# Down of two feed-forward layers by one step of Strassen's algorithm

## The chip, the cores and the metric

The kernel runs on one core of one Trainium2 chip. Its five queues of instructions are TensorE (PE, matrix products into PSUM; PEld is its loading of the stationary operand), VectorE (DVE), ScalarE (ACT), GpSimd (POOL) and SyncE (SP). In this kernel SP issues all DMAs, in the order in which the program has them, and an issue that has to wait for another engine or a transfer holds up those behind it. The metric is the time of one execution on the device in microseconds (us), as the median of several executions.

## The reference

Two layers on 1024 tokens of 1024 features, all in float32. Each layer has a token mixer (layer 0 forgetting attention, layer 1 an S5 state space) and a feed-forward part, each inside two RMSNorms:

```python
x = x + rmsnorm(m, mix_post_gain[i])
h = rmsnorm(x, ffn_pre_gain[i])
x = x + rmsnorm(swiglu(h, ffn_w_gate[i], ffn_w_up[i], ffn_w_down[i]), ffn_post_gain[i])

def swiglu(h, w_gate, w_up, w_down):
    return (jax.nn.silu(h @ w_gate) * (h @ w_up)) @ w_down
```

D_FF is 2816, that is 22 blocks of 128. The last product, g @ w_down, is what the change rewrites: 1024 tokens x 2816 features times 2816 x 1024, once per layer.

## The kernel before

**Precision.** A float32 operand is split in two of type fp32r: a rounded part h, written by ACT (`split`, L253), and the rest l = x - h, by DVE (L254). A product is then three matmuls, h*h, h*l and l*h (`mm3`, L270 to L274), each 128 x 128 stationary by 128 x 512 moving into one of eight PSUM banks.

**Loading ahead.** The operands that come from DRAM stand in one list (`plan`): source, shape, and the rings of pages that the parts go to. `take` returns an item's parts; it splits (`_cut`) the item taken and the next one, and each split sends the loads of the two items behind it (`_load`, L231). A ring is a short list of 4 KB pages in SBUF that are used in turn, so a load waits until its page's last reader is done. `raw` holds weights before the split (three pages in Down), `gr` the loaded g (two pages), `wdh`/`wdl` and `gh`/`gl` the parts. The order on each engine is not that of the code: a scheduler sets it from priorities and its own costs when the program is built, so SP's order, too, is one that it chose.

**gate_up** computes g = silu(h Wg) * (h Wu), transposed (features on partitions, tokens along the row), for two feature blocks 2p and 2p + 1 at a time. It takes them as the two halves of a Strassen step of its own with 14 steps of 12 matmuls (L756). The pages `s` hold g's blocks (z[0]) and `up` the partial sums (z[1]). After steps 11 and 13 the two blocks go to the DRAM tensor g_d (L813, L815).

**Down** (L825) runs over the two token halves (hf). In each it goes through the 11 pairs of feature blocks: the pair's two weight blocks of 128 x 1024 and its g (128 x 2 x 512) are taken, and for each of four token blocks tb and two column halves three matmuls per feature block add into bank 2 tb + nh. That is 48 matmuls a pair, 1056 a layer. The last two pairs are taken together, so that the four token blocks end one after another; ACT and DVE copy a block's two banks to a page m (L838, L839), and `finish` is called on it: `fin0` in layer 0 (norm, residual, store to x2, and the next norm's rstd; L1464 to L1473), `fin1` in layer 1 (a product with the gain, rstd, and one operation that scales and adds the residual x, which is loaded from x3, L1510; L1518 writes x and L1519 stores it to the output).

**Beside Down of layer 0.** `s5_rot` makes eight rotation tables for layer 1's mixer on POOL: per table six products (L1119 to L1121) on one page s5w0 and a scratch page s5w1, and a store to rot_d by SP (L1109). One table's code stands beside each of the first eight groups of the first half. Ahead of them `s5_params` does its last work beside gate_up; its last store, T_d (L1051), goes out from the scratch page that the first rot writes next. In the second half Down also takes eight rows of s5_w_in, which ACT and POOL split (L1224, L1225). After Down come `s5_in`'s transposes of the finished blocks (L1236).

Of the kernel before, what the change touches and what calls it, by code (L numbers as in the profile page):

```python
# [9 lines left out]
F32 = mybir.dt.float32  # L10
# [149 lines left out]
class Trunk:  # L160
    def __init__(self, ctx, tc, A, out):
        self.tc, self.nc, self.A, self.out = tc, tc.nc, A, out
        nc = self.nc
        mk = lambda name, bufs, **k: ctx.enter_context(tc.tile_pool(name=name, bufs=bufs, **k))
        self.cst = mk("cst", 1)
        self.hp = mk("hp", 4)
        self.pp = mk("pp", 1)
        self.sm = mk("sm", 4)
        self.ps = mk("ps", 1, space=bass.MemoryType.PSUM).tile([P, 8 * 512], F32, name="ps")
# [119 lines left out]
    def rstd(self, src, junk, cuts=1, out=None):  # L289
        nc = self.nc  # L290
        V = nc.vector
        ss, n = self.small("ss"), D // cuts
        for i in range(cuts):
            s = slice(i * n, i * n + n)
            part = self.small("sp") if i else ss
            nc.scalar.activation(junk[:, s], src[:, s], AF.Square, accum_out=part)
            if i:
                V.tensor_add(ss, ss, part)
# [389 lines left out]
    def ffn_plan(self, i, g_d, extra=()):  # L688

        A = self.A  # L690
        Wg, Wu, Wd = A["ffn_w_gate"][i], A["ffn_w_up"][i], A["ffn_w_down"][i]
        for p in range(NF // 2):
            for W in (Wg, Wu):
                for f in (2 * p, 2 * p + 1):
                    self.plan(self.cols(W, f * P)[:2] + (None, None, None))
        for hf in range(2):
            for p in range(NF // 2):
                for f in (2 * p, 2 * p + 1):
                    self.plan(self.rows(Wd, f * P, ("wdh", "wdl")))
                src = g_d[2 * p * P:(2 * p + 2) * P, hf * 512:hf * 512 + 512].rearrange("(a p) t -> p a t", p=P)  # L700
                self.plan((src, (P, 2, 512), ("gh", "gl"), None, None, "gr"))
                if hf:
                    self.plan(*extra[p:p + 1])

    def gate_up(self, B, g_d, beside=iter(()), when=lambda p, s: False):

# [63 lines left out]
        for p in range(n):  # L770
# [11 lines left out]
            for s in range(14):  # L782
# [42 lines left out]
    def down(self, finish, beside=iter(()), extra=0, last=2):  # L825
# [3 lines left out]
        nc, R = self.nc, self.R  # L829
        n = NF // 2  # L830
        groups = [[p] for p in range(n - last)] + [list(range(n - last, n))]
        for hf in range(2):
            m = {}

            def out(tb):
                t = m[tb] = R("m")
                with self.tc.high_priority(AHEAD):
                    nc.scalar.copy(t[:, 0:512], self.bank(2 * tb, 1, (P, 512)))  # L838
                    nc.vector.tensor_copy(t[:, 512:1024], self.bank(2 * tb + 1, 1, (P, 512)))  # L839

            for ps in groups:
                w = []
                for p in ps:
                    w.append((self.take(), self.take()))
                    w[-1] += (self.take(),)
                for tb in range(4):
                    t = slice(tb * P, tb * P + P)
                    for p, (w0, w1, g) in zip(ps, w):
                        for f, (wh, wl) in enumerate((w0, w1)):
                            for nh in range(2):  # L850
                                c = slice(nh * 512, nh * 512 + 512)
                                self.mm3(self.bank(2 * tb + nh, 1, (P, 512)), g[0][:, f, t], g[1][:, f, t], wh[:, c],
                                         wl[:, c], p == f == 0, p == n - 1 and f == 1)
                    if len(ps) > 1:
                        out(tb)
                if hf == 0:
# [519 lines left out]
def trunk(ctx: ExitStack, tc: tile.TileContext, A, out):  # L1376
# [36 lines left out]
    g_d = [T.dram(f"g{i}_d", [FF, D]) for i in range(2)]  # L1413
# [13 lines left out]
    R.set(pw=[29], R1=[30], R2=[31], s5t0=[34], s5t1=[32], s5t2=[33], s5w0=[28], s5w1=[32], fx=[4, 33], fj=[6, 34],  # L1427
# [34 lines left out]
    ys = []  # L1462

    def fin0(tb, m):  # L1464
# [8 lines left out]
        ys.append((m, T.rstd(m, R("fj"), out=T.rr5[:, tb:tb + 1])))  # L1473
# [12 lines left out]
    ins = [T.s5_in(tb, *ys[tb]) for tb in range(8)]  # L1486
# [34 lines left out]
    T.down(fin1)  # L1521
# [29 lines left out]
```

## Time and profile before

| | us |
|---|---|
| median of 3 runs | 2506.91 (2504.44 to 2507.9) |
| the profiled execution | 2504.19 |
| its span | 2502.4 |
| mean granted TensorE clock | 0.994 of full speed |

The busy time of each engine and its count of instructions stand in the page's first part, which the next section shows. In a window's line each engine has its busy time and, in brackets, how many of its instructions the window holds; then come the granted TensorE clock, the mean busy share of the 16 DMA engines and GB/s. In a group of instructions, busy time and mean ns stand behind the first bar, and behind the second the idle time ahead of them with what ended it. In the waits, an engine's line, what it waited for, total us, number of times and the longest. "SPq" rows are issues of DMAs.

### The profile page before, as it was taken

To read this page: it belongs to the slowest core of one execution; us is meant where nothing else is said; L and a number is where in the kernel's file an instruction comes from. 1 tells how busy PE (TensorE), PEld (TensorE's weight loads), DVE (VectorE), ACT (ScalarE), POOL (GpSimd) and SP (SyncE) were. 2 spreads that over 40 slices of the span, in tenths; PEclk is the share of its full clock that TensorE was granted. 3 is DMA by queue.
4 is the path that set the end of the run, shared out by engine and by line. 5 is a ranking of instruction groups with operands and counts; after the bars stand their busy time and mean duration, and the time that the engine had idled before them with its cause. 6 is when DMAs were issued, how large, how long until landed. Compare 5 with 4: busy or idle time off the path is not lost.

```text
span 2502.4 us, 31357 instructions
## 1 busy us (share of the span) xinstructions
PE 2421.5 (97%) x11748; PEld 1984.6 (79%) x11748; DVE 1576.0 (63%) x2803; ACT 1153.7 (46%) x1951; POOL 545.2 (22%) x447
## 2 busy tenths in 40 slices
PE   7999999999998999999999999899999999999998
PEld 5777777777787888888777878788878888888887
DVE  6877787778778865656536355763785554543444
ACT  5766676666655334343316343332453333332322
POOL 3323321223100035465782102420000000000100
PEclk9999999999999999999999999999999999999999
DMA  4121111211343323333547622443323223235452
GB/s 131 49 59 43 43 43 51 59 43 43 109 145 85 110 81 116 114 99 105 186 162 255 210 76 83 144 153 112 127 84 100 84 76 93 85 104 177 156 203 93
DMA packets 228872, 268.35 MB, mean 107 GB/s; under 512 B 31392, under 2 KB 176992, under 8 KB 228720
## 3 DMA queue, kind: packets, MB, share of 16 engines
q1 hardware_dynamic: 228720, 266.35, 33.3%
q8 instruction: 92, 1.51, 0.2%
q14 instruction: 60, 0.49, 0.1%
HBM read 205.95 MB, written 60.36 MB: 106 GB/s over the span
## 4 chain that ended last, share of the span: by engine, by line
PE 72%; DVE 12%; ACT 6%; POOL 5%; DMA 2%; issue 2%; SPq 0%; DVEq 0%; ACTq 0%; POOLq 0%
PE ps L756 30%; PE ps L272 11%; PE ps L273 11%; PE ps L274 11%; PE ps L567 2%; PE ps L586 1%; DVE wl L254 1%; DVE ps L548 1%; POOL s5w L1066 1%; DVE ptl L571 1%; DMA T_d<-s5w 1%; DVE p L434 1%; POOL s5w L1121 1%; POOL s5w L1120 1%; ACT pth L570 1%
## 5 line engine op out<-in xcount | busy, mean ns | idle before, releaser
L756 PE MATMUL ps<-B,ah 128*128 128x512 f32 x1056 | 329.4, 393 | 2.0 <-ACT hold L106 1.6
L273 PE MATMUL ps<-wdl,gh 128*128 128x512 f32 x704 | 275.0, 391 | 2.9 <-DVE wdl L254 2.9
L272 PE MATMUL ps<-wdh,gh 128*128 128x512 f32 x704 | 274.1, 390 | 3.0 <-ACT wdh L253 3.0
L274 PE MATMUL ps<-wdh,gl 128*128 128x512 f32 x704 | 274.2, 390 | 1.2 <-DVE gl L254 1.2
L254 DVE TENSOR_TENSOR wdl<-raw,wdh 128x1024 fp32r<-128x1024 f32 x88 | 119.7, 1362 | 219.1 <-ACT wdh L253 213.0
L756 PEld LDWEIGHTS ps<-B,ah 128*128 128x128 f32 x1056 | 200.3, 190 | 45.1 <-ACT hold L106 1.8
L756 PE MATMUL ps<-ops,ah 128*128 128x512 f32 x704 | 218.1, 391 | 0.0
L272 PE MATMUL ps<-hT,wh 128*128 128x512 f32 x512 | 207.2, 405 | 9.1 <-DVE pt L409 4.3
L555 POOL TENSOR_SCALAR Pt<-Pt,ri 128x128 f32<-128x128 f32 (+7 forms) x128 | 118.2, 925 | 414.7 <-DVE ri L554 326.3
L756 PE MATMUL ps<-B,al 128*128 128x512 f32 x528 | 207.0, 392 | 0.0
L253 ACT CAST wdh<-raw 128x1024 fp32r<-128x1024 f32 x88 | 92.5, 1051 | 248.1 <-PE ps L274 163.4
L273 PE MATMUL ps<-hT,wh 128*128 128x512 f32 x512 | 203.5, 397 | 0.0
L274 PE MATMUL ps<-hT,wl 128*128 128x512 f32 x512 | 202.7, 396 | 0.0
L1514 POOL TENSOR_TENSOR y<-m,s 128x1024 f32<-128x1024 f32 x6 | 15.3, 2552 | 817.1 <-DVE m L839 812.8
L273 PEld LDWEIGHTS ps<-wdl,gh 128*128 128x128 f32 x704 | 132.5, 188 | 31.8 <-DVE wdl L254 4.3
L272 PEld LDWEIGHTS ps<-wdh,gh 128*128 128x128 f32 x704 | 132.6, 188 | 31.7 <-ACT wdh L253 3.9
L274 PEld LDWEIGHTS ps<-wdh,gl 128*128 128x128 f32 x704 | 132.6, 188 | 29.0 <-DVE gl L254 1.7
L756 PEld LDWEIGHTS ps<-ops,ah 128*128 128x128 f32 x704 | 131.4, 188 | 28.8 <-issue 1.7
L727 DVE TENSOR_TENSOR al<-raw,ah 128x1024 fp32r<-128x1024 f32 x88 | 117.8, 1339 | 52.6 <-ACT ah L726 52.1
L726 ACT CAST ah<-raw 128x1024 fp32r<-128x1024 f32 x88 | 92.6, 1052 | 125.6 <-PE ps L756 114.6
L571 DVE TENSOR_TENSOR ptl<-ps,pth 128x512 fp32r<-128x512 f32 (+1 forms) x192 | 106.3, 554 | 54.9 <-ACT pth L570 49.6
L756 PE MATMUL ps<-ops,al 128*128 128x512 f32 x352 | 137.0, 389 | 0.0
(322 smaller groups left out, 5645.2 us busy)
## 6 DMA issues: line engine op xcount, KB each, us to landing
raw<-in_ffn_w_down_dram SPq DMA_DIRECT2D x88, 512.0 KB, 4.6
raw<-in_ffn_w_gate_dram SPq DMA_DIRECT2D x44, 512.0 KB, 3.9
raw<-in_ffn_w_up_dram SPq DMA_DIRECT2D x44, 512.0 KB, 4.3
g_d<-s SPq DMA_DIRECT2D x44, 512.0 KB, 3.4
gr<-g_d SPq DMA_DIRECT2D x44, 512.0 KB, 5.2
raw<-in_fox_w_in_dram SPq DMA_DIRECT2D x32, 512.0 KB, 4.2
x<-in_x_dram SPq DMA_DIRECT2D x16, 512.0 KB, 6.2
An<-negc SPq DMA_DIRECT2D x16, 512.0 KB, 4.7
```

The source lines that it names most:

```text
L253: self.nc.scalar.copy(h, src)
L254: self.lsub.tensor_sub(l, src, f32(h))
L272: mm(ps, lh, rh, start=start, stop=False)
L273: mm(ps, lh, rl, start=False, stop=False)
L274: mm(ps, ll, rh, start=False, stop=stop)
L434: nc.vector.tensor_sub(l, qs[r], f32(h))
L555: nc.gpsimd.tensor_scalar(p[:, :nk], p[:, :nk], ri, 1.0, op0=ALU.mult, op1=ALU.mult)
L567: nc.tensor.transpose(p2[:, i], p[:, (g + i) * P:(g + i + 1) * P], self.ident)
L571: nc.vector.tensor_sub(dl, p2[:, 0:n], f32(dh))
L726: nc.scalar.copy(h, src)
L727: V.tensor_sub(l, src, f32(h))
L756: nc.tensor.matmul(bank, x[:, k], y, start=start and k == i == 0, stop=True, skip_group_check=True)
```

## The change

The sum over 22 blocks is cut in halves (blocks p and p + 11), and so are tokens and columns; of the eight half products seven are left, in Winograd's form. gate_up now takes blocks p and p + 11 as its pair and stores, besides parts of g itself, the sums and differences that the seven products need: g_d becomes four DRAM tensors. Down runs four phases. The first three take two products at a time, X in the even banks and Y in the odd ones, 24 matmuls a pair; the fourth takes the last product alone, on Y, two pairs at a time (24 matmuls again, the last step one pair). 7 x 132 = 924 matmuls a layer. Between phases ACT and DVE move sums from PSUM to the eight pages m; X goes on adding through the first three phases. The differences of weights are made on DVE from raw rows (`sums`): three 128 x 512 operations a pair in the second phase, two in the third. The `rot` code stands beside every second pair of the first phase and the steps of the fourth; the s5_w_in rows are taken in the third.

```diff
-        for p in range(NF // 2):
+        n = NF // 2
+        for p in range(n):
             for W in (Wg, Wu):
-                for f in (2 * p, 2 * p + 1):
+                for f in (p, p + n):
                     self.plan(self.cols(W, f * P)[:2] + (None, None, None))
-        for hf in range(2):
-            for p in range(NF // 2):
-                for f in (2 * p, 2 * p + 1):
-                    self.plan(self.rows(Wd, f * P, ("wdh", "wdl")))
-                src = g_d[2 * p * P:(2 * p + 2) * P, hf * 512:hf * 512 + 512].rearrange("(a p) t -> p a t", p=P)
-                self.plan((src, (P, 2, 512), ("gh", "gl"), None, None, "gr"))
-                if hf:
-                    self.plan(*extra[p:p + 1])
...
+            def cut(raw):
+                b = self.cut[-1]
+                t, h, l = self.R("t"), self.R("wdh", sh, F32R), self.R("wdl", sh, F32R)
+                if second:
+                    V.tensor_sub(t[:, hi], b[:, hi], b[:, lo])
+                    V.tensor_sub(t[:, lo], raw[:, hi], t[:, hi])
+                    V.tensor_sub(t[:, hi], raw[:, lo], t[:, lo])
+                else:
+                    V.tensor_sub(t[:, lo], raw, b[:, hi])
+                    V.tensor_sub(t[:, hi], b[:, hi], b[:, lo])
+                self.split(h, l, t.rearrange("p (a c) -> p a c", a=2))
+                return h, l
...
+        for p in range(n):
+            ga(0, p)
+            self.plan((W2[p][:, :, lo], sh, op, None, None))
+        for p in range(n):
+            ga(1, p)
+            self.plan(rows(p), rows(p + n)[:2] + (sums(1, 1), None, None))
+        for p in range(n):
+            ga(2, p)
+            self.plan(rows(p), (W2[p][:, 1, hi], (P, 512), sums(1, 0), None, None), *extra[p:p + 1])
+        for p in range(0, n, 2):
+            ga(3, p)
...
                 elif s == 11:
                     times(0, hi)
-                    nc.sync.dma_start(g_d[2 * p * P:2 * p * P + P, :], z[0][0])
+                    g0, g1, q0, q1 = *z[0], *z[1]
+                    V.tensor_add(q0[:, hi], g0[:, hi], g1[:, hi])
+                    V.tensor_sub(q0[:, lo], g0[:, lo], g0[:, hi])
+                    nc.sync.dma_start(g_d[0][p][:, lo], g0[:, lo])
+                    nc.sync.dma_start(g_d[1][p][:, hi], g1[:, hi])
+                    nc.sync.dma_start(g_d[2][p], q0)
                 elif s == 13:
-                    nc.sync.dma_start(g_d[2 * p * P + P:2 * p * P + 2 * P, :], z[0][1])
+                    V.tensor_sub(q1[:, lo], q0[:, hi], g0[:, lo])
+                    V.tensor_sub(q1[:, hi], g1[:, lo], q1[:, lo])
+                    nc.sync.dma_start(g_d[0][p][:, hi], g1[:, lo])
+                    nc.sync.dma_start(g_d[1][p][:, lo], q1[:, lo])
+                    nc.sync.dma_start(g_d[3][p], q1[:, hi])
...
+        for ph in range(3):
+            for p in range(n):
+                g = self.take()
+                if ph:
+                    self.take()
+                w = self.take()
+                for tb in range(4):
+                    mm(X[tb], g, w, 0, tb, p == ph == 0)
+                    mm(Y[tb], g, w, 1, tb, p == 0)
+                if ph == 2 and p < extra:
+                    self.take()
+                if ph == 0 and p % 2 == 0:
+                    next(beside, None)
+            with self.tc.high_priority(AHEAD):
+                for tb in range(4):
+                    a, b = m[tb], m[4 + tb]
+                    if ph == 0:
+                        nc.scalar.copy(a[:, lo], X[tb])
+                        V.tensor_add(a[:, lo], a[:, lo], Y[tb])
...
+        for tb in range(4, 8):
+            finish(tb, m[tb])
+        js = list(range((n + 1) // 2))
+        for i, grp in enumerate([[j] for j in js[:-last]] + [js[-last:]]):
+            ops = [(self.take(), self.take()) for j in grp]
+            next(beside, None)
+            for tb in range(4):
+                for j, (g, w) in zip(grp, ops):
+                    for k in range(min(2, n - 2 * j)):
+                        mm(Y[tb], g, w, k, tb, False)
+                if len(grp) > 1:
+                    with self.tc.high_priority(AHEAD):
+                        V.tensor_add(m[tb][:, hi], m[tb][:, hi], Y[tb])
+                    finish(tb, m[tb])
...
-    R.set(raw=[0, 1, 2], gr=[35, 36], gh=[3, 37, 18], gl=[5, 7, 29], wdh=rg(8, 13), wdl=rg(13, 18), m=rg(19, 27), s=[27])
-    T.down(fin0, T.s5_rot(), 8)
+    R.set(raw=[0, 1, 2, 14], gr=[35, 36], t=[15, 16], gh=[3, 37, 18], gl=[5, 7, 29], wdh=rg(8, 11), wdl=rg(11, 14),
+          m=rg(19, 27), s=[27])
+    T.down(fin0, beside=T.s5_rot(), extra=8)
...
-    R.set(raw=[0, 1, 2], gr=[32, 33], gh=[35, 36, 37], gl=[7, 8, 9], wdh=rg(10, 15), wdl=rg(15, 19) + [20], m=rg(22, 30))
+    R.set(raw=[0, 1, 2, 19, 20], gr=[32, 33, 14], t=[15, 16], gh=[35, 36, 37], gl=[7, 8, 9], wdh=rg(10, 13) + [17],
+          wdl=[13, 18, 21, 34], m=rg(22, 30), x=[3, 4], y=[5, 6], y4=[5, 6, 15, 16], j=[31], s=[30])
```

In layer 1 a new `begin1` computes the first column half of the last four blocks' gain product (POOL) and square sum (ACT) ahead of their end; fin1 then does the second half, with the gain product on POOL for blocks 4 to 7 and on DVE for 0 to 3, and x and its store in two halves for block 3, which now ends last. Blocks 4 to 7 are finished beside the fourth phase, in both layers, and s5_in takes the blocks in that order.

Three places of the built program follow. The first is SP's queue where gate_up of layer 0 ends and Down begins. A name's number grows with the place in the code, so of the g loads before the change gr_10865 is pair 0's and gr_10883, gr_10958 and gr_11033 those of pairs 1 to 3. Before:

```order
L231 DMA gr_10865<-g_d 128x2x512
L813 DMA g_d<-s_10606 128x1024
L231 DMA gr_10883<-g_d 128x2x512
L1051 DMA T_d<-s5w_1034_10840 128x1024
L231 DMA raw_11027<-in_ffn_w_down_dram 128x1024
L815 DMA g_d<-s_10607 128x1024
L231 DMA raw_10952<-in_ffn_w_down_dram 128x1024
L1109 DMA rot_d<-s5w_1049_10933 128x1024
L231 DMA gr_10958<-g_d 128x2x512
```

Now, where gr_10962, gr_10970, gr_10982 and gr_11027 are pairs 0, 1, 2 and 3:

```order
L857 DMA g_d<-up_10698 128x512
L1118 DMA T_d<-s5w_1034_10933 128x1024
L232 DMA gr_10970<-g_d 128x1024
L856 DMA g_d<-s_10696 128x512
L858 DMA g_d<-up_10698 128x512
L335 DMA s_12415<-in_ffn_post_gain_dram 128x1024
L1176 DMA rot_d<-s5w_1054_11008 128x1024
L232 DMA gr_10962<-g_d 128x1024
L232 DMA gr_11027<-g_d 128x1024
L1176 DMA rot_d<-s5w_1068_11089 128x1024
L232 DMA gr_10982<-g_d 128x1024
L1176 DMA rot_d<-s5w_1082_11170 128x1024
```

The loads of pairs 0 and 3 now stand behind the first rot store, pair 2's behind the second; in the rows that follow each further rot store is followed by the g load of one pair, 4 to 9, and the eighth also by the first weight row of the second phase, raw_11381. Pair 0's page (35) is also that of up_10698, so its load stands behind L857 and L858 in any case.

The second place is DVE at the end of that first phase, where before it only went on with splits (gl and wdl, L254). gl_11267 and wdl_11297 are pair 8's, t_11430 is the second phase's first difference. Now:

```order
L255 TENSOR_TENSOR wdl_11261<-raw_11219,wdh_11260 128x1024
L255 TENSOR_TENSOR gl_11267<-gr_11225,gh_11266 128x1024
L709 TENSOR_TENSOR t_11430<-raw_11381 128x512
L255 TENSOR_TENSOR wdl_11297<-raw_11264,wdh_11296 128x1024
L255 TENSOR_TENSOR gl_11303<-gr_11270,gh_11302 128x1024
```

The difference L709, which needs raw_11381, is ahead of pair 8's wdl.

The third place is SP's queue at the very end, stores of finished blocks (out_dram) and loads of x. Before, with x_19836 for the last block and x_19818 for the one ahead of it:

```order
L1510 DMA x_19818<-x_d 128x1024
L1519 DMA out_dram<-x_19800 128x1024
L1510 DMA x_19836<-x_d 128x1024
L1519 DMA out_dram<-x_19818 128x1024
L1519 DMA out_dram<-x_19836 128x512 x2
```

and now, with x_20195 for the last block and x_20161 for the one ahead:

```order
L1584 DMA x_20161<-x_d 128x1024
L1591 DMA out_dram<-x_20127 128x1024
L1591 DMA out_dram<-x_20161 128x1024
L1584 DMA x_20195<-x_d 128x1024
L1591 DMA out_dram<-x_20195 128x512 x2
```

The last block's x load has moved behind the store of the block ahead of it.

More of the change, by code (lines that the diff above doesn't have):

```diff
@@ L286, in new_hT, with rstd @@
                 for _ in range(2)]
-    def rstd(self, src, junk, cuts=1, out=None):
+    def rstd(self, src, junk, part=None, out=None):
         nc = self.nc
         V = nc.vector
[L292 to L298, printed above, removed]
+        ss = self.small("ss")
+        s = slice(0 if part is None else 512, D)
+        nc.scalar.activation(junk[:, s], src[:, s], AF.Square, accum_out=ss)
+        if part is not None:
+            V.tensor_add(ss, ss, part)
         rt = self.small("rt")
@@ new lines, in ffn_plan, with rows, sums @@
+        V, sh, lo, hi, op = self.nc.vector, (P, 2, 512), slice(0, 512), slice(512, 1024), ("wdh", "wdl")
+        def rows(r):
+            return (Wd[r * P:r * P + P, :], (P, D), None, None, None)
+        def sums(first, second):
+            def cut(raw):
[10 more added lines that the diff above has]
+                return h, l
+            return cut
@@ new lines, in ga @@
+        def ga(x, k0=None):
+            src = g_d[x][k0].rearrange("p (a c) -> p a c", a=2) if x < 3 else g_d[3][k0:min(k0 + 2, n)].rearrange("k p c -> p k c")
+            m = src.shape[1]
+            self.plan((src, (P, m, 512), ("gh", "gl"), None, None, "gr"))
+        for p in range(n):
[4 more added lines that the diff above has]
+            self.plan(rows(p), rows(p + n)[:2] + (sums(1, 1), None, None))
@@ L823, in gate_up, with down @@
                     next(beside, None)
-    def down(self, finish, beside=iter(()), extra=0, last=2):
+    def down(self, finish, begin=lambda tb, m: None, beside=iter(()), extra=0, last=3):
         nc, R = self.nc, self.R
+        V = nc.vector
         n = NF // 2
[L831 to L845, printed above, removed]
-                for tb in range(4):
[L847 to L856, printed above, removed]
-                    next(beside, None)
-                elif ps[0] < extra:
-                    self.take()
-            for tb in range(4):
-                finish(4 * hf + tb, m[tb])
@@ new lines, in down, with mm @@
+        lo, hi = slice(0, 512), slice(512, 1024)
+        m = {tb: R("m") for tb in (4, 5, 6, 7, 0, 1, 2, 3)}
+        X, Y = ([self.bank(2 * tb + i, 1, (P, 512)) for tb in range(4)] for i in (0, 1))
+        def mm(bank, g, w, j, tb, start):
+            t = slice(tb * P, tb * P + P)
+            for i, (x, y) in enumerate(((g[0], w[0]), (g[0], w[1]), (g[1], w[0]))):
+                nc.tensor.matmul(bank, x[:, j, t], y[:, j], start=start and i == 0, stop=True, skip_group_check=True)
+        for ph in range(3):
[4 more added lines that the diff above has]
+                w = self.take()
+                for tb in range(4):
+                    mm(X[tb], g, w, 0, tb, p == ph == 0)
[3 more added lines that the diff above has]
+                if ph == 0 and p % 2 == 0:
+                    next(beside, None)
+            with self.tc.high_priority(AHEAD):
[4 more added lines that the diff above has]
+                        V.tensor_add(a[:, lo], a[:, lo], Y[tb])
+                    elif ph == 1:
+                        nc.scalar.copy(a[:, hi], X[tb])
+                        V.tensor_copy(b[:, lo], Y[tb])
+                    else:
+                        nc.scalar.copy(b[:, hi], Y[tb])
+                        V.tensor_add(b[:, lo], b[:, lo], X[tb])
+                        V.tensor_add(b[:, hi], b[:, hi], X[tb])
@@ new lines, in down @@
+        for tb in range(4, 8):
[4 more added lines that the diff above has]
+            next(beside, None)
+            for tb in range(4):
+                for j, (g, w) in zip(grp, ops):
[5 more added lines that the diff above has]
+                    finish(tb, m[tb])
+            if i == 0:
+                for tb in range(4):
+                    begin(tb, m[tb])
@@ L864, in exp @@
+        run(beside)
     def exp(self, x, out, tmp):
@@ L1412, in trunk @@
     T.plan(*wos[:4], T.cols(Wi, 3 * D + 7 * P), act[0], *wos[4:], *act[1:])
-    g_d = [T.dram(f"g{i}_d", [FF, D]) for i in range(2)]
+    g_d = [[T.dram(f"g{i}{x}_d", [NF // 2, P, D if x < 3 else 512]) for x in range(4)] for i in range(2)]
     T.ffn_plan(0, g_d[0], [T.rows(A["s5_w_in"][0], k * P, T.s5_w_in_cut(k)) for k in range(8)])
@@ L1460, in trunk @@
     gp = []
-    ys = []
+    ys = {}
     def fin0(tb, m):
@@ L1472, in fin0 @@
         nc.sync.dma_start(x2_d[:, tb, :], m)
-        ys.append((m, T.rstd(m, R("fj"), out=T.rr5[:, tb:tb + 1])))
+        ys[tb] = m, T.rstd(m, R("fj"), out=T.rr5[:, tb:tb + 1])
     R.widen("raw", 19)
@@ L1481, in trunk @@
     T.slots = (0, 2)
-    R.set(raw=[0, 1, 2], gr=[35, 36], gh=[3, 37, 18], gl=[5, 7, 29], wdh=rg(8, 13), wdl=rg(13, 18), m=rg(19, 27), s=[27])
-    T.down(fin0, T.s5_rot(), 8)
+    R.set(raw=[0, 1, 2, 14], gr=[35, 36], t=[15, 16], gh=[3, 37, 18], gl=[5, 7, 29], wdh=rg(8, 11), wdl=rg(11, 14),
+          m=rg(19, 27), s=[27])
+    T.down(fin0, beside=T.s5_rot(), extra=8)
     T.U = [R("U", (P, 8, 8, 16)) for _ in range(8)]
     T.tab, T.st, T.M, T.pe = {}, {}, [], None
-    ins = [T.s5_in(tb, *ys[tb]) for tb in range(8)]
+    ins = [T.s5_in(tb, *ys[tb]) for tb in (4, 5, 6, 7, 0, 1, 2, 3)]
     run(T.s5_tables(0))
```

31 lines of the change are left out of this document (18 added, 13 removed).

## The prediction

> **What bounds the kernel now.** I read the page first, then the two stages that the change rewrites, as windows, then who waited there.
>
> ```profile
> span 2502.4 us, 31357 instructions
> PE 2421.5 (97%) x11748; PEld 1984.6 (79%) x11748; DVE 1576.0 (63%) x2803; ACT 1153.7 (46%) x1951; POOL 545.2 (22%) x447
> 1220.80:1470.70 249.90, 242.72 (x1058) 199.06 (x1058) 126.45 (x137) 92.37 (x124) 103.49 (x64) 0.99 0.56 192
> 2255.00:2494.00 239.00, 239.00 (x1055) 197.58 (x1054) 95.70 (x106) 76.19 (x89) 15.31 (x6) 1.00 0.46 156
> ```
>
> PE is the bound, and the two windows are Down of layer 0 and of layer 1. A matmul is listed with some 390 ns, but these overlap: layer 1 puts 1055 of its 1056 into 239.0 us, so one costs 0.2267 us. At that pitch Down takes 239.4 us. Layer 1 reaches that; layer 0 takes 249.9, 10.5 more. SP's queue and POOL say why:
>
> ```profile
> SPq L1109 <- POOL s5w L1121: 65.5, 8, 9.7
> 1232.02 0.32 SPq L1109 DMA_DIRECT2D rot_d<-s5w  x1
> 1232.43 0.39 SPq L231 DMA_DIRECT2D gr<-g_d  x1
> ...
> 1285.71 0.32 SPq L1109 DMA_DIRECT2D rot_d<-s5w  x1
> 1286.13 0.37 SPq L231 DMA_DIRECT2D raw<-in_ffn_w_down_dram  x1
> ...
> 1304.91 0.32 SPq L1109 DMA_DIRECT2D rot_d<-s5w  x1
> 1286.13 4.41 DMA raw<-in_ffn_w_down_dram
> ...
> 1293.88 0.80 PE ps L273
> ```
>
> The eight rot stores wait at SP's head for POOL, 65.5 us in total, and loads written behind them go out 0.4 us after each: at 1286.13 a weight row left behind the sixth store, landed 4.41 us later, was split, and PE waited for it until 1293.88. POOL sets the stores' pace: first at 1232.0, eighth at 1304.9, one per 10.4 us.
>
> ```profile
> L1120 POOL TENSOR_TENSOR s5w<-R,R 128x512 f32<-128x512 f32 x16 | 30.1, 1907 | 2.7 <-DMA T_d<-s5w 2.1
> L1121 POOL TENSOR_TENSOR s5w<-s5w,s5w 128x512 f32<-128x512 f32 x16 | 29.2, 1845 | 0.0
> L1119 POOL TENSOR_TENSOR s5w<-R,R 128x512 f32<-128x512 f32 x16 | 24.1, 1527 | 9.3 <-issue 8.3 <-DMA rot_d<-s5w 1.1
> ```
>
> Before the change a pair of feature blocks is 48 matmuls, 10.9 us, about one rot: POOL just kept up.
>
> **What is removed.** 132 matmuls per layer (924 for 1056): 132 x 0.2267 = 29.9 us, 59.9 in both, if everything else stays covered. A pair now takes 24 matmuls, 5.44 us.
>
> **Layer 0, first phase.** The rots stay as they are, 83 us of POOL from 1218 on, but this phase wants only 11 x 5.44 = 59.8 us. By SP's order the load of pair 0's g stands behind the first rot store, those of pairs 2, 4, 5, 6, 7, 8 and 9 behind the next seven, and the first weight row of the second phase behind the last; and DVE has that row's difference ahead of pair 8's wdl. POOL's start isn't moved: it waits for the T_d store, which stands behind stores that need only step 11. So I keep the measured stores. Pair 0 would start thus:
>
> ```profile
> 1215.34 0.38 SPq L231 DMA_DIRECT2D gr<-g_d  x1
> 1219.67 1.05 ACT L253 CAST gh<-gr 128x1024 fp32r<-128x1024 f32 x1 [0.38 <-DMA gr<-g_d]
> 1220.75 2.41 DVE L254 TENSOR_TENSOR gl<-gr,gh 128x1024 fp32r<-128x1024 f32 x1
> 1223.22 0.50 PE L274 MATMUL ps<-wdh,gl 128*128 128x512 f32 x1 [1.25 <-DVE gl L254]
> ```
>
> From issue to PE 7.9 us: 1232.4 + 7.9 = 1240.3, where PE was ready at 1220.8. Pairs 4 to 7 then come one per rot, with a gap of some 4 us each. Pair 8 waits for the weight row behind the eighth store: 1304.9 + 0.8 issue + 4.6 landing + 0.7 difference + 1.2 split = 1312.2. After such gaps the granted clock falls:
>
> ```profile
> 1294.00:1295.00 1.00, 1.00 (x3) 0.81 (x4) 1.00 (x1) 0.00 (x0) 0.96 (x1) 0.50 0.00 0
> ...
> 1296.00:1297.00 1.00, 1.00 (x3) 0.75 (x3) 0.05 (x1) 0.00 (x0) 1.00 (x1) 0.50 0.99 393
> ```
>
> Half clock for 3.5 us costs 1.7 us; it counts only at pair 8, since earlier PE waits anyway. Pair 8 ends at 1312.2 + 5.2 + 1.7 = 1319.1, pairs 9 and 10 at 1330.0. The phase takes 109.2 us instead of 59.8. Ends: the chain of work shows POOL's shortest pieces,
>
> ```profile
> 1279.41 2.79 POOL s5w L1119 x2
> 1282.21 3.49 POOL s5w L1121 x2
> ```
>
> and with a third like the first a rot takes 9.1 us, so the eighth comes 9 us earlier; were each as much longer than 10.4 as the shortest is shorter, it comes 9 later. What stands behind a waiting rot store is thus all that feeds PE: SP's next g and weight rows, behind them ACT's casts, and on DVE a pair's wdl behind its gl.
>
> **The later phases.** DVE does three subtractions and two splits per pair in the second:
>
> ```profile
> L744 DVE TENSOR_TENSOR raw<-raw,raw 128x512 f32<-128x512 f32 x21 | 14.5, 691 | 0.7
> L254 DVE TENSOR_TENSOR wdl<-raw,wdh 128x1024 fp32r<-128x1024 f32 x43 | 52.7, 1225 | 125.0 <-ACT wdh L253 124.9
> ```
>
> 3 x 0.69 + 2 x 1.22 = 4.5 us of 5.44, so PE covers it. ACT's two casts need 2.1 (1.05 each above). What gets tight is transfers: 1.57 MB a pair is 289 GB/s, and in layer 0's third phase, with s5_w_in, 1.84 MB is 337 GB/s.
>
> ```profile
> 1310.00:1320.00 10.00, 10.00 (x45) 8.00 (x44) 4.27 (x4) 4.20 (x4) 0.00 (x0) 1.00 0.98 333
> DMA packets 10696, 29.60 MB, mean 247 GB/s; under 512 B 1907, under 2 KB 1907, under 8 KB 10689
> ```
>
> Ten microseconds at 333 have been seen, with PE full; a mean over 1300 to 1420 is 247, though not because more was wanted. I take 289 as carried, and 337 as just missed: 2 us (0 to 10). At layer 0's first phase boundary DVE reaches the sums out of PSUM only after differences whose rows were loaded late: 3 us (0 to 6). The fourth phase has fin0 of four blocks beside its splits:
>
> ```profile
> L1470 DVE SCALAR_TENSOR_TENSOR m<-m,rr,s 128x1024 f32<-128x1024 f32 x4 | 5.1, 1285 | 0.1
> L1471 DVE TENSOR_TENSOR m<-fx,m 128x1024 f32<-128x1024 f32 x4 | 4.9, 1222 | 0.1
> ```
>
> With 0.7 for the sum and 1.9 of 128x1 work that is 5.1 us a block. By DVE's order two blocks stand ahead of the last split, which comes just in time: 1 us (0 to 6). In the last group PE needs 15 x 0.2267 = 3.4 us a block, so DVE runs late into s5_in: 1 us (-2 to 4), since four blocks are done early and PE can begin with them.
>
> The Trainium skill, "DMA: Bandwidth & Descriptors", section "Bandwidth", speaks against this change: it wants 1 MiB a transfer for three quarters of the peak. By the page's fit (section "Anatomy of one DMA — SWDGE (gpsimd) path": 2.0 us plus bytes over 436 GB/s) I estimate 3.2 us for 512 KB; three in turn would be 9.6 us a pair, and by that the sum would be some 90 us worse. The row with 333 GB/s, from 512 KB transfers, says that they overlap.
>
> Layer 0: 109.2 + 62.8 + 61.8 + 30.9 = 264.7 against 249.9, so +14.8, +1 for s5_in.
>
> **Layer 1.** There is no POOL work beside it, five raw pages and three for g, so prefetch is deeper: -29.9 + 1.5 (0 to 8). The end:
>
> ```profile
> 2494.42 0.39 PE L274 MATMUL ps<-wdh,gl 128*128 128x512 f32 x1
> 2495.40 0.68 DVE L839 COPY m<-ps 128x512 f32<-128x512 f32 x1
> ...
> 2498.04 1.41 DVE L1518 SCALAR_TENSOR_TENSOR x<-y,rr,x 128x512 f32<-128x512 f32 x2
> x<-x_d SPq DMA_DIRECT2D x16, 512.0 KB, 3.6
> x<-x_d SPq DMA_DIRECT2D x4, 512.0 KB, 4.7
> ```
>
> From the last matmul's end (2494.7) to the span's end were 7.7 us. Now a block in the last group takes PE 3.4 us, but DVE 2.6 (2495.4 to 2498.0) + 1.3 for a whole x (its halves take 1.4) = 3.9. Counted from PE's end, PE gives blocks at -10.2, -6.8, -3.4 and 0; DVE ends two at -6.3 and -2.4, has the third's rr at +0.2, sums the fourth (0.7) and ends the third at +2.2. SP has tb 3's x load behind that store: +0.5, landing 3.6 (of all) to 4.7 (of this stage), two halves 1.4, and 3.0 from there to the end as now: 10.7 to 11.8. So +3 (0 to 4). Layer 1 in all: -25.4.
>
> **gate_up.** Four more 128x512 DVE operations a pair, 2.8 us in 38, and 1.8 MB stored for 1.0.
>
> ```profile
> 1841.00:2255.00 414.00, 413.55 (x1813) 341.88 (x1813) 226.67 (x291) 149.11 (x206) 0.00 (x0) 0.99 0.29 90
> ```
>
> In layer 1's gate_up DVE is 55% and DMA 29% busy beside a full PE, which covers both: 0 (-1 to 4, if q0's store holds the page that step 1 of the next pair writes).
>
> **Sum.** +14.8 + 1 - 25.4 = -9.6. The profiled execution took 2504.2 (span 2502.4), so 2494.6; the median of the runs shown is 2506.9, 2.7 above it: **2497**.
>
> **Rivals.** *The loads aren't held*: rots come sooner, or SP reaches the g loads ahead of them. Pair 0 still waits for its page, on which the last g stores leave at 1222.5: it starts at 1233.8. Layer 0 then ends near 1451, 20 us earlier than now, and the time is 2504.2 - 19.7 + 1 - 25.4 + 2.7 = 2463. Against it stand the 65.5 us of waiting above. *Transfers become the bound, and it is slower*: second phases carry 17.3 MB each, layer 0's third 18.6. At 247 GB/s they take 70.0, 70.0 and 75.3 us instead of 59.8 each, 36 more, of which 3.5 are counted: 2530. For it: in-order issue and few pages (layer 0's half rows wait for the page that the previous sums free). Against: 333 GB/s above. It decides below 276 GB/s, where 53.2 MB take 192.5 us and the gain of 9.6 is gone. *DVE as the bound*: stretched by the 22% that POOL costs it, 5.5 us a pair, hardly over PE.
>
> **How the numbers follow.** The forecast has 74%, free loads 11%, bound transfers 15%. The forecast's own bounds, not all at one end, give 2478 to 2518; what lies outside is nearly all of both rivals, so I leave that as the range. About 0.2%, 5 us, can be told from no change: under 2502 is faster, over 2512 slower. The forecast splits 50, 18 and 6; free loads add 11 to faster, bound transfers 14 to slower and 1 to same: 0.61, 0.19, 0.20.
>
> **What would show it.** Right: in layer 0's first phase PE about half busy, idle from 1221 to some 1240, SP waiting for POOL at each rot store; Down 0 some 265 us and Down 1 some 211; granted clock 0.5 in slices of that phase; the last x load issued after PE has ended. Wrong: phase 0 near 60 us (free loads); or PE waiting for raws in second and third phases at a DMA share near 0.75 (bound transfers); or waits for wdl with DVE full.

## The result and the profile after

| kernel | median us (lowest to highest) | ratio to before, 95% interval | profiled execution, its span |
|---|---|---|---|
| before | 2506.94 (2504.44 to 2507.90) | | 2504.19, 2502.4 |
| after | 2492.68 (2489.97 to 2494.28) | 0.9944 [0.9926, 0.9961] | 2489.97, 2488.2 |

The change makes the kernel 14.3 us faster, 0.56%. The two profiled executions differ by 14.2 us as well, so their stages can be compared. First the page of after, its span and its engines:

```profile
span 2488.2 us, 31505 instructions
PE 2369.5 (95%) x11484; PEld 1940.4 (78%) x11484; DVE 1729.9 (70%) x3053; ACT 1177.0 (47%) x1989; POOL 532.3 (21%) x449
```

The 264 matmuls are gone (11748 before), and PE is busy 52 us less; yet only 14 us are won, so some 38 us of new idle time must be found. The windows of both Downs (length, then busy time and count of PE, PEld, DVE, ACT and POOL, clock, DMA share, GB/s):

```profile
1223.70:1478.50 254.80, 220.35 (x926) 179.31 (x925) 169.11 (x187) 99.64 (x125) 98.85 (x64) 0.92 0.67 231
2262.10:2473.50 211.40, 210.09 (x925) 173.03 (x923) 150.29 (x183) 87.08 (x110) 17.86 (x8) 1.00 0.70 233
```

Layer 1 does 924 matmuls in 211.4 us, 2 over the 209.5 that the pitch gives. Layer 0 takes 254.6 from PE's last gate_up matmul to the first transpose of s5_in, 45 over, with the clock at 0.92. From PE's timeline at the stages' ends:

| stage | before | after | difference | forecast |
|---|---|---|---|---|
| to the end of gate_up 0 | 1220.9 | 1223.9 | +3.0 | 0 |
| Down 0 | 249.7 | 254.6 | +4.9 | +14.8 |
| s5 mixer to the end of gate_up 1 | 784.5 | 783.6 | -0.9 | +1 |
| Down 1, to the last matmul | 239.65 | 211.4 | -28.25 | -28.4 |
| last matmul to the span's end | 7.6 | 14.65 | +7.05 | +3 |
| sum | | | -14.2 | -9.6 |

Where Down 0 stands, by the view of waits of SP's queue (total, times, longest) and SP's timeline, first and last of the eight stores:

```profile
SPq L1176 <- POOL s5w L1188: 64.5, 8, 9.8
```

```profile
1232.31 0.32 SPq L1176 DMA_DIRECT2D rot_d<-s5w  x1
1232.74 1.20 SPq L232 DMA_DIRECT2D gr<-g_d  x2
1241.48 0.32 SPq L1176 DMA_DIRECT2D rot_d<-s5w  x1
...
1302.21 0.32 SPq L1176 DMA_DIRECT2D rot_d<-s5w  x1
```

and on PE's timeline the matmuls that waited (in brackets: how long, for whom):

```profile
1238.32 0.80 PE L883 MATMUL ps<-wdh,gh 128*128 128x512 f32 x1 [14.38 <-ACT gh L254]
...
1290.08 0.50 PE L883 MATMUL ps<-wdh,gh 128*128 128x512 f32 x1 [2.65 <-ACT wdh L254]
1293.39 0.80 PE L883 MATMUL ps<-wdl,gh 128*128 128x512 f32 x1 [2.81 <-DVE wdl L255]
1310.83 0.80 PE L883 MATMUL ps<-wdl,gh 128*128 128x512 f32 x1 [9.69 <-DVE wdl L255]
```

The stores still wait 64.5 us at SP's head (65.5 before), one per 10.0 us, loads go out right behind each, and PE's waits end at 1310.83 with pair 8's wdl. From there 731 matmuls end at 1478.5, in 167.7 us for 165.7 at the pitch. The lower clock just after that wait, 0.53 of full speed from 1310 to 1315, makes up most of the 2 us, so the later phases lose next to nothing.

### The profile page after: what moved, and what is told of

The parts are those of the page before. It is cut to its first block, busy times and chain, and to the rows that moved or that the text cites. A ratio compares the mean times of both kernels' runs of the same rounds, so it can differ in the third digit from the quotient of the medians.

```text
span 2488.2 us, 31505 instructions
## 1 busy us (share of the span) xinstructions
PE 2369.5 (95%) x11484; PEld 1940.4 (78%) x11484; DVE 1729.9 (70%) x3053; ACT 1177.0 (47%) x1989; POOL 532.3 (21%) x449
## 4 chain that ended last, share of the span: by engine, by line
PE 53%; DVE 4%; POOL 3%; DMA 2%; ACT 2%; issue 1%; SPq 0%; DVEq 0%; POOLq 0%; ACTq 0%
PE ps L790 28%; PE ps L883 14%; PE ps L275 3%; PE ps L273 3%; PE ps L274 3%; POOL s5w L1188 1%; POOL s5w L1186 1%; DMA rot_d<-s5w 1%; PE ps L1268 0%; PE ps L1226 0%; PE ps L1267 0%; POOL s5w L1187 0%; DVE y L315 0%; ACT fj L296 0%; DMA x<-x_d 0%
## 5 line engine op out<-in xcount | busy, mean ns | idle before, releaser
L883 PE MATMUL ps<-wdh,gh 128*128 128x512 f32 x616 | 243.5, 395 | 17.2 <-ACT gh L254 14.4
L883 PE MATMUL ps<-wdl,gh 128*128 128x512 f32 x616 | 243.8, 396 | 16.6 <-DVE wdl L255 16.6
L883 PE MATMUL ps<-wdh,gl 128*128 128x512 f32 x616 | 243.1, 395 | 2.0 <-DVE gl L255 2.0
L254 ACT CAST gh<-gr 128x1024 fp32r<-128x1024 f32 (+1 forms) x78 | 81.1, 1040 | 233.8 <-DMA gr<-g_d 86.4
L255 DVE TENSOR_TENSOR gl<-gr,gh 128x1024 fp32r<-128x1024 f32 (+1 forms) x78 | 103.6, 1329 | 111.9 <-ACT gh L254 111.9
L1576 POOL TENSOR_TENSOR y<-m,s 128x512 f32<-128x512 f32 x4 | 7.3, 1823 | 767.4 <-DMA raw<-in_ffn_w_down_dram 757.0
L761 DVE TENSOR_TENSOR al<-raw,ah 128x1024 fp32r<-128x1024 f32 x88 | 111.8, 1270 | 61.9 <-ACT ah L760 61.5
L883 PEld LDWEIGHTS ps<-wdl,gh 128*128 128x128 f32 x616 | 117.9, 191 | 43.1 <-DVE wdl L255 18.3
L883 PEld LDWEIGHTS ps<-wdh,gh 128*128 128x128 f32 x616 | 117.7, 191 | 42.9 <-ACT gh L254 14.8
L883 PEld LDWEIGHTS ps<-wdh,gl 128*128 128x128 f32 x616 | 117.8, 191 | 27.7 <-DVE gl L255 3.1
L570 ACT CAST pth<-ps 128x512 fp32r<-128x512 f32 (+1 forms) x192 | 91.9, 479 | 95.6 <-PE ps L567 83.5
```

The lines of the kernel that those rows point to most:

```text
L254: self.nc.scalar.copy(h, src)
L255: self.lsub.tensor_sub(l, src, f32(h))
L570: nc.scalar.copy(dh, p2[:, 0:n])
L761: V.tensor_sub(l, src, f32(h))
L883: nc.tensor.matmul(bank, x[:, j, t], y[:, j], start=start and i == 0, stop=True, skip_group_check=True)
```

## Experiments

Down 0 is counted as above; what it has over 209.5 us, 924 matmuls at the pitch, is lost. All runs are of the changed kernel, except the two called before. The median is of four or five executions, Down 0 of the profiled one alone: that one was the slowest of its four in rot_m_pool (2485.14) and the fastest in after (2489.97), so a median and a Down 0 can differ by a few us in what they say.

| run | median us, ratio to before [interval] | Down 0, us |
|---|---|---|
| rot_pool | 2496.89, 0.9963 [0.9948, 0.9978] | 260.3 |
| before_rot_pool | 2518.83, 1.0046 [1.0031, 1.0061] | 260.7 |
| rot_m_pool | 2482.73, 0.9904 [0.9889, 0.9918] | 245.4 |
| before_rot_m_pool | 2498.05, 0.9964 [0.9950, 0.9979] | 241.8 |
| rot_m_gr | 2483.29, 0.9908 [0.9893, 0.9923] | 246.8 |
| no_rots | 2468.88, 0.9843 [0.9827, 0.9860] | 229.6 |
| early_rots | 2550.91, 1.0176 [1.0161, 1.0191] | 227.1 |
| early_rots_gr | 2545.11, 1.0155 [1.0139, 1.0172] | 222.2 |
| no_q | 2483.40, 0.9908 [0.9891, 0.9924] | 246.2 |
| x_pages | 2489.54, 0.9930 [0.9915, 0.9945] | 253.9 |
| x_pages_3 | 2489.34, 0.9931 [0.9917, 0.9946] | 254.2 |
| rots_dve | 2475.43, 0.9883 [0.9867, 0.9900] | 241.1 |

**The rot stores off SP's queue** (rot_pool, and before_rot_pool on the kernel before):

```diff
-            self.nc.sync.dma_start(self.rot_d[ch], rot.rearrange("p i a b c -> p (i a b c)"))
+            self.nc.gpsimd.dma_start(self.rot_d[ch], rot.rearrange("p i a b c -> p (i a b c)"))
```

> The changed kernel, with the eight rot stores issued by POOL itself instead of by SP, so that no load stands behind them. Theory (loads held behind the rot stores): SP no longer waits for POOL, layer 0's first Down phase shrinks from 104.9 us to 60 to 75 (pair 0 still waits for its page until the last g stores, so PE starts near 1234), Down 0 takes 225 to 240 us instead of 254.8, and the time falls by 15 to 28 us to 2465 to 2478. Rival 1 (POOL's own work beside DVE, or the casts, hold the first phase): the phase stays at 95 us or more and the time within 4 us of 2492.7. Rival 2 (transfers): the first phase shrinks, but PE then waits for raw and gr in the second phase, and less than half of the 15 to 28 us is left.

> The kernel before, with the same one edit (rot stores issued by POOL). Theory: its layer 0 Down loses its 10.5 us over the pitch, to 239 to 242 us, so the time falls by 7 to 11 us to 2496 to 2500; and the gap between this and the changed kernel with the same edit is 22 to 35 us, more than the 14 of the change as it stands. Rival (the 10.5 us come from POOL's and DVE's work): within 3 us of 2506.9.

Both came out slower, by 4 and 12 us. In rot_pool, the waits of SP's queue and, on PE's timeline, the one long wait:

```profile
SPq L1206 <- POOL M L1202: 38.6, 1, 38.6
```

```profile
1322.14 0.80 PE L883 MATMUL ps<-wdl,gh 128*128 128x512 f32 x1 [32.61 <-DVE wdl L255]
```

PE ran without a gap from 1240 to 1289, as the theory wants; then SP reached the first load of M, which waits for a memset that stands behind all eight rots on POOL, and everything behind it stood until 1312. The short holds had become one long one (of 45.6 us in before_rot_pool). The queue is still the cause; the edit moved only one of two kinds of transfers that wait for POOL.

**Both kinds off SP** (rot_m_pool and before_rot_m_pool):

```diff
-            dma(M[j * 16:j * 16 + 16, :, s * 16:], KT[:, :, 0:P - s * 16])
+            (dma if ch else self.nc.gpsimd.dma_start)(M[j * 16:j * 16 + 16, :, s * 16:], KT[:, :, 0:P - s * 16])
```

> The changed kernel with both kinds of transfers that wait for POOL taken off SP in layer 0's Down: the eight rot stores as in the run before, and the eight loads of the first M as well, which wait for a memset that stands behind all rots on POOL; POOL issues them. In the run with the rot stores alone SP's head stood 38.6 us at the first of these loads and PE 32.6 us behind it, after nine pairs at full pace. Theory (SP's head is held by whatever waits for POOL): no wait of SP for POOL over 3 us in the first phase, the phase takes 70 to 78 us from the end of gate_up (start near 1236, 59.8 of matmuls), Down 0 takes 222 to 230 us instead of 254.8, the time is 2462 to 2470. Rival (the store of rots was only the first of several bounds; loads through two pages of g, or DVE's order, hold PE next): the first phase stays over 90 us and the time over 2480.

> The kernel before with the same two edits. Theory: layer 0's Down falls from 249.9 us to 239 to 242, the time to 2496 to 2500. Then the change itself, without the held loads on either side, is worth 28 to 36 us, about twice the 14.2 measured. Rival: the time stays within 3 us of 2507, so that the kernel before lost nothing to the held loads that isn't lost to something else.

For the kernel before, the theory holds: 2498.05, Down 0 at 241.8, 2.4 over its pitch. For the changed kernel a third of the gain came: 2482.73, and Down 0 still 36 over. The change is then worth 15.3 us, hardly more than as it stands, not 28. In rot_m_pool PE now waits elsewhere (view of waits of PE, Down 0), and the groups of DVE between 1300 and 1332 say why (count, busy us, mean ns):

```profile
PE ps L883 <- ACT gh L254: 10.8, 1, 10.8
PE ps L883 <- DVE m L903: 8.9, 1, 8.9
PE ps L883 <- DVE m L906: 3.3, 1, 3.3
```

```profile
L711 DVE TENSOR_TENSOR t<-raw,t 128x512 f32<-128x512 f32 x5 | 7.4, 1481 | 0.1
...
L255 DVE TENSOR_TENSOR wdl<-t,wdh 128x1024 fp32r<-128x1024 f32 x3 | 5.5, 1819 | 0.0
...
L903 DVE TENSOR_TENSOR m<-m,ps 128x512 f32<-128x512 f32 x4 | 2.6, 674 | 0.0
```

While POOL computes rots, DVE's differences take 1.48 us and its splits 1.82; the sum that reads PSUM keeps its 0.67. The second phase needs three differences and two splits a pair, 8.1 us at these means against 5.44 of PE: DVE is the bound wherever rots and the second phase overlap. In the same trace POOL's last product ends at 1327.6, and from 1329 on DVE's splits take 1.21 us and its differences 0.69 again. As the change stands, the two do not overlap: PE's waits for loads stretch the first phase until POOL is done, at 1302.1.

**Without the rots' products** (no_rots):

```diff
-            self.prod(G, rot[:, 0], e1(0), e2(0), e1(1), e2(1), ALU.subtract, k[:, 0])
-            self.prod(G, rot[:, 1], e1(0), e2(1), e1(1), e2(0), ALU.add, k[:, 1])
+            G.memset(rot, 0.0)
```

> The changed kernel with its rot stores on SP, but without the rots' products: a memset of the page stands in their place, so the tables of the S5 mixer are of zeros. This takes POOL's 83 us out of layer 0's Down, and with them both the held loads and the slow-down of DVE. Theory (the two together are all that the change lost in layer 0; with transfers off SP alone DVE's 128x512 operations took 1.4 to 1.5 us instead of 0.69 while POOL ran, and PE stood 8.9 us for sums out of PSUM): Down 0 takes 222 to 230 us instead of 254.8, the time 2460 to 2470. Rival (a third thing, such as pages or transfers, bounds phases 1 and 2 of layer 0): Down 0 stays over 238 us and the time over 2478.

The groups of DVE in the same window, for no_rots:

```profile
L255 DVE TENSOR_TENSOR wdl<-t,wdh 128x1024 fp32r<-128x1024 f32 x6 | 7.3, 1217 | 0.0
...
L711 DVE TENSOR_TENSOR t<-raw,t 128x512 f32<-128x512 f32 x6 | 4.1, 690 | 0.2
L903 DVE TENSOR_TENSOR m<-m,ps 128x512 f32<-128x512 f32 x4 | 2.6, 679 | 0.0
```

The theory holds: 2468.88 and 229.6. So POOL's rots cost the changed kernel 25 us of Down 0 (254.6 - 229.6): 9.2 come back when transfers leave SP, the other 15.8 only when POOL's work goes. By the medians the two together are 23.8 us. What stays, 20 us over the pitch, begins with 12.0 of waiting for pair 0's g. That wait was 14.4 us in after, and 11.6 in rot_pool and 10.8 in rot_m_pool, which have no rot store on SP: only some 2 to 4 us of it were the rot store's.

**That first wait** (rot_m_gr, and early_rots_gr below): `gr=[35, 36]` becomes `gr=[36, 35]` in layer 0's Down.

> As the run with both kinds of transfers on POOL, and besides with the two pages of the ring for g in layer 0's Down in the other order, so that pair 0's g takes the page that is free sooner and pair 1's the one that the last g stores leave. Theory (the rest of PE's wait at the start of Down is for that page, and for the load through it): the first Down matmul moves from near 1236 to between 1228 and 1233, and the time falls by another 3 to 8 us. Rival (pair 0's g can't be loaded sooner, as its store is itself late, or pair 1 waits instead): within 2 us of the run without it.

The first wait falls from 10.8 to 5.7 us, the time not at all: PE comes earlier to a DVE that is still late. A wait ahead of an engine that is the bound was worth nothing here.

**The rots earlier** (early_rots, early_rots_gr), on top of both transfers on POOL:

```diff
-    T.gate_up(B, g_d[0], T.s5_params(), lambda p, s: s in first.get(p, (5, 12)))
+    s5 = chain(T.s5_params(), T.s5_rot())
+    T.gate_up(B, g_d[0], s5, lambda p, s: s in first.get(p, (3, 7, 12)))
```

> The changed kernel with the same work, but the steps of S5's parameters spread over gate_up at three a pair instead of two, the rots behind them in the same list, so that POOL has done all or most of them before Down starts; POOL issues the rot stores and the first M loads. Theory: in gate_up DVE has room (69% busy at most) and PE loses under 4 us there, Down 0 is then free of POOL and takes 222 to 230 us, the time is 2460 to 2470. Rival 1 (POOL's chain of parameters can't be done faster than one chunk a pair, since it waits for PE, ACT and its own stores): the rots still run into Down and the time is over 2478. Rival 2 (DVE slowed by POOL holds PE in gate_up instead): gate_up 0 grows by 8 us or more.

> As the run with the early rots, with the two pages of the ring for g in layer 0's Down in the other order. Theory: where nothing else stands in the way, the page of the last g stores is what PE waits for at the start of Down, so the first matmul comes 3 to 6 us sooner and the time falls by as much. Rival (as in the first run with this edit, pair 1 waits instead): within 2 us of the run without it.

What is left of the list at the end of gate_up would go on in Down, but nothing was left. POOL's last products of the rots:

```profile
1248.99 3.97 POOL L1189 TENSOR_TENSOR s5w<-s5w,s5w 128x512 f32<-128x512 f32 x2
```

Down 0 is 227.1, as the theory says, but gate_up 0 ends at 1310.9 instead of 1223.9. So rival 2 came true, and of rival 1 the time over 2478, but not the rots in Down. Waits of PE in gate_up 0, and a group of DVE between 1160 and 1250, where POOL is busy for 77 of the 90 us:

```profile
PE ps L1147 <- POOL s5w L1134: 27.6, 14, 5.0
PE ps L791 <- DVE al L762: 22.5, 3, 9.5
```

```profile
L762 DVE TENSOR_TENSOR al<-raw,ah 128x1024 fp32r<-128x1024 f32 x5 | 18.1, 3627 | 0.0
```

PE's own matmuls for the parameters waited for POOL, and a DVE split took 3.63 us in the mean, three times its 1.22; the longest took 9.30. With the pages swapped, nothing else stands in the way in Down 0, and PE's first wait falls from 9.9 to 4.6 and Down 0 by 4.9. Here the wait for the page is time: the median falls by 5.8 us, though the intervals overlap.

**The sums q** (no_q; the four sums per pair in gate_up are left out):

> The changed kernel without the four sums q per pair of gate_up in both layers: what q0 and q1 held before is stored in their place, with the same stores and loads, so the products of Down are of other numbers. Theory (the sums' time on DVE makes gate_up longer): layer 0's gate_up ends near 1221 instead of 1223.7, layer 1's takes 425.3 instead of 427.2, and the time falls by 3.5 to 6 us. Rival (the larger stores or the wait for their pages do): both stay as they are, time within 1.5 us.

The time fell by 9.3 us, more than the theory asked, and for another reason: the mixer and gate_up 1 take 783.6 us with and without them, so the sums cost DVE nothing that PE feels in layer 1. In layer 0 gate_up ends at 1222.9 instead of 1223.9, where the theory had 1221. The gain is in Down 0, 246.2 us instead of 254.6, by SP's timeline of no_q:

```profile
1228.48 0.32 SPq L232 DMA_DIRECT2D gr<-g_d  x1
1234.57 0.32 SPq L1172 DMA_DIRECT2D rot_d<-s5w  x1
```

Three g loads, of which this is the last, stand ahead of the first rot store now, where after has one (at 1222.74). The first Down matmul comes at 1227.3 instead of 1238.3, and PE waits 4.4 us for it instead of 14.4. Neither expectation names that.

**The end** (x_pages; x_pages_3 with `raw=[0, 1, 2, 19]` and `x=[3, 4, 20, 3, 4, 20, 1, 2]`):

```diff
-          wdl=[13, 18, 21, 34], m=rg(22, 30), x=[3, 4], y=[5, 6], ...
+          wdl=[13, 18, 21, 34], m=rg(22, 30), x=[3, 4, 3, 4, 3, 4, 1, 2], y=[5, 6], ...
```

> The changed kernel, with the last two x loads of the end put into pages 1 and 2, whose last weight rows are long used, so that these loads wait for no store. Theory (page ring of x with the store ahead of the load in SP's order): both are issued before PE's last matmul, tb 3 no longer waits for x, and the stretch from the last matmul's end to the span's end falls from 14.8 us to 9 to 11.5, the time by 3 to 6 us. Rival (DVE's chain of sum, square and scale is the bound): the loads are early, but the stretch stays at 13.5 or more and the time within 1.5 us of 2492.7.

> The changed kernel with x of the end in a ring of three pages for its first six loads (a weight page of layer 1's Down is given up for it: four raw pages instead of five) and in pages 1 and 2 for the last two. With the last two alone the stretch after PE's last matmul was 12.1 us instead of 14.8, and DVE stood 2.2 us for the x of the third phase's last block ahead of the sum of the first block of the last group. Theory: that wait goes too, the stretch becomes 9.5 to 10.8 us, the time 2486 to 2488.5. Rival (DVE's four blocks at 3.9 us each bound the end from PE's side, whatever x does): 12 us as before, 2489.5 or more. If four weight pages are too few, PE waits for wdl in layer 1's Down.

In after, DVE's timeline has two waits for x, and SP's has the last load behind a store:

```profile
2464.91 1.28 DVE L1590 SCALAR_TENSOR_TENSOR x<-y,rr,x 128x1024 f32<-128x1024 f32 x1 [2.33 <-DMA x<-x_d]
2466.11 0.68 DVE L923 TENSOR_TENSOR m<-m,ps 128x512 f32<-128x512 f32 x1
...
2483.59 1.41 DVE L1590 SCALAR_TENSOR_TENSOR x<-y,rr,x 128x512 f32<-128x512 f32 x2 [3.08 <-DMA x<-x_d]
```

```profile
2474.52 4.71 SPq L1591 DMA_DIRECT2D out_dram<-x  x2
2479.33 0.38 SPq L1584 DMA_DIRECT2D x<-x_d  x1
```

x_pages takes away the second (3.1 us): the stretch is 12.05 us instead of 14.65, just outside the theory's 9 to 11.5, and the median is 3.1 lower. The intervals of the two overlap; it is the trace that shows the gain. x_pages_3 takes away the first too, and its stretch is 8.9; but PE's last matmul comes 2.5 us later in Down 1, behind DVE, and the time is that of x_pages. The view of waits of PE in its Down 1:

```profile
PE ps L883 <- DVE gl L255: 2.5, 2, 1.8
```

So the second wait for x was time, and taking the first away by this edit gained nothing: DVE has the third phase's blocks and the last splits to do either way, and four blocks at 3.9 us each bound the end. The rival is right beyond the first 3 us. Whether the raw page that x_pages_3 gives up has a part in PE's later end was not tried alone.

**The version that the runs point to** (rots_dve; with both transfers on POOL and x as in x_pages):

```diff
 def s5_rot(self):
-        R, sh, G = self.R, (P, 4, 8, 16), self.nc.gpsimd
+        R, sh, G = self.R, (P, 4, 8, 16), self.nc.vector
```

> The changed kernel with all of its work, and three edits that the runs point to: the eight rots are computed by DVE instead of POOL (48 operations of 128x512, some 33 us at 0.69 us each if they cost what DVE's other 128x512 operations do, into a phase in which a pair leaves DVE 3 us of 5.44), the rot stores and first M loads are issued by POOL, and the last two x loads of the end have pages 1 and 2. Theory (held loads, and DVE slowed while POOL computes, are what layer 0's Down loses): without either, Down 0 takes 225 to 235 us instead of 254.8 and the time is 2463 to 2474, near the run without the rots' products less 3 us for x. Rival (DVE, now with 33 us more in the first phase, becomes the bound there): Down 0 stays over 240 us and the time over 2480.

At 2475.43 it beats the kernel before by 1.17% and the changed one by 17 us, with the whole computation done. It stands 1.4 us over the theory's range, and Down 0, at 241.1, is over the mark set for the rival. Its groups of DVE from 1215 to 1320:

```profile
L1187 DVE TENSOR_TENSOR s5w<-R,R 128x512 f32<-128x512 f32 x16 | 17.0, 1096 | 0.5 <-DMA T_d<-s5w 0.3
L1186 DVE TENSOR_TENSOR s5w<-R,R 128x512 f32<-128x512 f32 x16 | 16.9, 1100 | 3.2 <-DMA rot_d<-s5w 3.0 <-issue 0.2
L255 DVE TENSOR_TENSOR wdl<-raw,wdh 128x1024 fp32r<-128x1024 f32 x11 | 13.3, 1220 | 0.8 <-ACT wdh L254 0.8
...
L1188 DVE TENSOR_TENSOR s5w<-s5w,s5w 128x512 f32<-128x512 f32 x16 | 10.6, 686 | 0.0
```

The splits are back at 1.22 us. But the products of two broadcast tables take 1.10 instead of the 0.69 that I had put, so the rots take 44.5 us of DVE and not 33, and PE still waits 4.9 us for the sums of the first phase: both theory and rival have a part.

## Why the prediction came out as it did

The measured 2492.7 lies 4.3 under the forecast and within its own bounds. That the total is so near is in part luck: of the stages, Down 0 was put 9.9 us too dear and the mixer with gate_up 1 1.9, gate_up 0 3.0 and the end 4.0 too cheap. Point by point:

- **What is removed** held: 924 matmuls a layer, and layer 1 at 211.4 us to the last matmul, 28.25 less for 28.4 forecast.
- **The rot stores hold layer 0's first phase**: right in kind and nearly in size. PE idle from 1223.9 to 1238.3 (forecast: from 1221 to 1240.3), pair 8 at 1310.8 (1312.2), stores one per 10.0 us (10.4), clock 0.50 from 1230 to 1240. The first of these waits, though, is mostly that for pair 0's page: the forecast's rival, in which the page alone is left, had 13.0 us for it (1233.8 - 1220.8), and 11.6 and 10.8 of the 14.4 stay when no rot store is on SP.
- **The later phases of layer 0** were put 6 us too dear. No stall came at the boundary, in the third phase or in the fourth. Windows of after with PE full:

```profile
1350.00:1360.00 10.00, 10.00 (x46) 8.29 (x45) 8.30 (x10) 4.01 (x4) 0.00 (x0) 1.00 0.97 351
...
1420.00:1430.00 10.00, 10.00 (x46) 8.29 (x45) 8.98 (x10) 4.85 (x5) 0.95 (x1) 1.00 0.93 330
```

- **gate_up 0** ended 3.0 us later, for 0 forecast; the way to pair 8 was not longer for it, so of the 9.9 us by which Down 0 was put too dear 3.0 are this later start, 1.4 pair 8, and the rest the later phases. The cause of the later end stays open. The trace says where the time is lost: between 790 and 1224 PE waits 2.1 us for cc (ACT, L1103), 1.4 for s (ACT, L830) and 1.0 for al (DVE, L761), none of which it does before, and no_q lacks all three. The stage also varies: it ended at 1225.2 in rot_pool, 1226.9 in x_pages and 1228.2 in no_rots, where the edits lie behind it.
- **The end** is the term that was mis-sized, +7 for +3 (0 to 4). The forecast let DVE begin the last group's first block when PE gives it, 10.2 us before PE's end. By the rows above it began at 2466.1, 7.4 before: ahead of it, in DVE's order, stood the third phase's last block, waiting for its x. From there each block took its 3.9 us, and so the last x load, which the forecast had counted at 2.7 us after PE's end, went out 5.8 after it.
- **The rival of free loads** was kept at 2463. Had it come, it would have been 20 us wrong: with the loads free the time is 2482.7. The step that fails is the aside that DVE would be hardly over PE, "stretched by the 22% that POOL costs it, 5.5 us a pair": the stretch is 50% for splits and 115% for differences, 8.1 us a pair. The 22% is near what the mean over the whole Down 0 of the kernel before gives (1.49 us for 1.22), but the rots fill only a third of that stretch. While they run a split took 1.96 there; from 1220.8 to 1470.7, then from 1225 to 1305:

```profile
L254 DVE TENSOR_TENSOR wdl<-raw,wdh 128x1024 fp32r<-128x1024 f32 x42 | 62.4, 1488 | 91.2 <-ACT wdh L253 87.6 <-PE ps L756 3.3
L254 DVE TENSOR_TENSOR wdl<-raw,wdh 128x1024 fp32r<-128x1024 f32 x11 | 21.6, 1964 | 30.8 <-ACT wdh L253 30.6
```

- **Bound transfers** did not come: 351 GB/s with PE full. The Trainium skill, "DMA: Bandwidth & Descriptors", section "Bandwidth", wants at least 1 MiB a transfer for three quarters of the peak. The trace does not agree: these are 512 KB transfers, issued one per 1.8 us and landing 5 us after issue, so several are in flight. The forecast's estimate of some 90 us by the page's fit counts the 22 pairs of the two second phases alone; the third phases, with 2.5 to 3.5 such transfers a pair, would have added to it.

So of the 59.9 us removed, some 46 were lost again: 35 in layer 0's Down (10 over its pitch before, 45 now), 7 at the end, 3 in gate_up 0, 1.6 in Down 1, less 0.9 between. Of the 45, no_rots shows 25 to be POOL's rots, through SP's queue and through DVE together; the waits of no_rots put 12 to pair 0's g, and the rest, among it the lower clock after that wait, was not taken apart.

## What to carry over

- Work that was hidden beside a long stage is no longer hidden when the stage shrinks: ask of each neighbour whether it fits the new length, here 83 us of POOL beside 60 of PE.
- An in-order queue that waits for a slow engine is cured only when everything on it that waits for that engine is moved; and behind the cure stands the next bound, so price a rival with the durations that will hold then, not with those of idle neighbours, and take them from the stretch in which the two engines overlap, not from a mean over the stage.
- At the end of a program, look at what stands ahead of the first block in the engine's order, not only at the rate of the blocks.

## What the hardware showed

DVE slows while POOL computes, and whether it does depends on the operands. 128x1024 splits go from 1.22 us to 1.82 in rot_m_pool, 1.96 in the kernel before, 2.32 in after (1240 to 1300) and 3.63 in early_rots, 128x512 differences from 0.69 to 1.48, while the sum with one operand in PSUM stays at 0.67 to 0.68. Why the means differ so stays open: POOL was about as busy in rot_m_pool (28 of 32 us) as in early_rots (77 of 90). The Trainium skill, "SBUF — State Buffer", section "Who interferes with whom", says that a DVE instruction with two SBUF inputs contends with a GpSimd instruction that reads SBUF, and one with at most one such input, outside the two-port modes, does not; the rows agree. And a 128x512 product of two broadcast tables took DVE 1.10 us where a sum or difference of plain operands takes 0.69; whether the broadcast or its strides cost that was not tried.
